# Two heads in one operand: mirrored odd heads in the level products of a recurrent mixer

## The chip, the cores and the metric

The kernel runs on one core of a Trainium2 chip. The time is the device time of one execution in microseconds (us); the figure compared is the median of several executions. The core has a matrix engine (TensorE, PE in the profile; its weight loads are PEld), a vector engine (VectorE, DVE), a scalar engine (ScalarE, ACT), GpSimd (POOL) and a queue engine that issues most transfers (SyncE, SP). Each works through its own instruction list in order and waits for the others by semaphores. TensorE reads its two operands from the on-chip memory (SBUF) and writes to the accumulators (PSUM), which DVE and ACT read.

## The reference

One inference step of a two-layer decoder: 1024 prompt tokens and 8 sample tokens share the weights, model width 1024, everything in float32. Layer 0 mixes tokens by a gated linear recurrence (HGRN2) with four heads of 128 beside cross-attention into 256 memory tokens, layer 1 by stick-breaking attention; each layer ends with a SwiGLU network of width 2816. The change touches the recurrence, whose prompt part is

```python
def a_mixer(hn, w_in, lb, hg_gain, mem_k, mem_v, w_o, s0):
    q_h, f_h, i_h, g_h, q_m = jnp.split(hn @ w_in, 5, axis=-1)
    q = jax.nn.silu(q_h).reshape(B, L, HG_HEADS, HG_DK)
    logf = jnp.logaddexp(jnp.log(lb), jnp.log1p(-lb) + jax.nn.log_sigmoid(f_h.astype(jnp.float32)))
    k = -jnp.expm1(logf)
    v = i_h.reshape(B, L, HG_HEADS, HG_DV)
    o, S = hgrn2_scan(q, k, v, logf, s0)
...
def hgrn2_scan(q, k, v, logf, s0):          # one step over a chunk
    b = jnp.cumsum(fi, axis=2)
    o_inter = jnp.einsum('bhtk,bhkv->bhtv', qi * jnp.exp(b), S)
    rel = b[:, :, :, None, :] - b[:, :, None, :, :]
    dec = jnp.exp(jnp.where(causal, rel, -jnp.inf))
    att = jnp.einsum('bhtk,bhsk,bhtsk->bhts', qi, ki, dec)
    o = o_inter + jnp.einsum('bhts,bhsv->bhtv', att, vi)
    S_new = jnp.exp(b_last[:, :, 0, :, None]) * S + jnp.einsum('bhsk,bhsv->bhkv', ki * jnp.exp(b_last - b), vi)
```

The score of a query at time t for a key at an earlier time s is a sum over 128 channels of q, k and the product of all forget gates f between s and t; each channel has gates of its own, so `att` is not one matrix product. After the mixer comes a norm per head and an output gate, then the output projection.

## The kernel before, in words

The prompt is done in two groups g of G = 512 tokens; the second also carries the 8 sample tokens (width WID = 520). Activations lie with channels on the 128 partitions and time along the free axis. A float32 projection (`proj`, L274) is three matmuls per weight block: weights are split into a rounded part (ACT, L260) and a remainder (DVE, L261), and rounded x rounded, rounded x remainder and remainder x rounded are summed. A projection of one head takes 8 weight blocks, so 24 matmuls of 512 columns.

The recurrence of a group is `hgrn_prompt` (called `core` of the mixer). The four heads go in two pairs hp; the tiles `Ft`, `Kt`, `Qt` hold gates, keys and queries of a pair, head hh = 0 or 1 in the middle index. A chunk is 128 time steps, CH = 4 of them in a group. First the diagonal of each chunk (L1160, four matmuls of 128 columns for each head, times the identity into the score tile `atts`). Then seven levels, lv = 0 to 6, with m = 1, 2, 4, ... 64: a chunk is cut into blocks of 2m, and the late half's queries meet the early half's keys, each already multiplied by the gates to the border between the halves. Only the late half's queries are read, 64 columns of a chunk, with a step. For one level and one pair these are 8 matmuls (L1180: two heads, four chunks) into one PSUM tile `s`. Afterwards DVE extends the products: late queries times the gate product of the early half (L1185), early keys times that of the late half (L1186), and the gate products of the merged blocks (L1187). `copy_predicated` (L1190) writes those rows of the PSUM tile that belong to the block into `atts`, under `mask`, one table for each level, which POOL makes at the kernel's start with two `affine_select` each (L163, L166) and DVE casts (L169).

The end of the core goes head by head ("tail" below): K is transposed (L1201), copied by ACT to `kT` (L1203), multiplied with V (L1207), chunk by chunk the scores meet V (L1215) and the carried state meets Q (L1219), while DVE moves the state on (L1220, L1224); then square (ACT, L1226), a sum over channels by a matmul with ones (L303), Ln and Exp on ACT (L304, L305), and the scaled output (DVE, L1228).

What else TensorE does meanwhile is set by `weave`: it takes generators with weights and steps the one that is furthest behind its weight. Group 0's core is woven with a chain: the memory tokens' load, keys (`mem_keys`, L812, transposes L820) and values (`mem_values`, L839, its splits L835 and L836) of layers 0 and 1, and last the memory queries `qm`, four projections of 24 matmuls, evacuated at L1232. Group 1's core is woven with a part of group 0's SwiGLU network. Tiles come from rotating pools (PSUM `s` 3 buffers, score and other tiles `b` 7, temporaries `t` 3, split weights `ws` 5), and a scheduler sets the final order of each engine's instructions within these dependences.

At the start (`start`, L373) four blocks of 128 tokens are loaded (`xtok`), DVE and ACT form sums of squares (L366 on DVE, L368 on ACT), ACT the reciprocal roots (L369, L370), DVE scales the block (L371), TensorE transposes it (L396) and ACT evacuates (L399). The first projection rows (L1048, splits at L1043) need all four blocks. The masks of POOL and DVE are made in the same microseconds, as are the page indices `pidx` (POOL, L207 and L208).

Of the kernel before, what the change touches and what calls it, by code (L numbers as in the profile page):

```python
# [9 lines left out]
F32 = mybir.dt.float32  # L10
# [14 lines left out]
def tile_decoder(  # L25
# [46 lines left out]
    def nm(s):  # L72
        uid[0] += 1
        return f"{s}_{uid[0]}"
# [62 lines left out]
    make_identity(nc, ident)  # L137
    ones = const.tile([P, P], F32, name="ones")
    nc.vector.memset(ones, 1.0)
    epsb = const.tile([P, 1], F32, name="epsb")  # L140
    nc.vector.memset(epsb, EPS)
    trif = const.tile([P, P], F32, name="trif")
# [11 lines left out]
        compare_op=ALU.is_equal, fill=0.0, base=0, channel_multiplier=0,  # L154
    )

    mask = const.tile([P, 7, 64], U8, name="mask")
    for lv in range(7):
        m = 1 << lv
        nb = 64 // m  # L160
        mf = tpool.tile([P, nb, m], F32, tag="t", name=nm("mf"))
        src = ones[:, 0:64].rearrange("p (b m) -> p b m", m=m)
        nc.gpsimd.affine_select(  # L163
            mf, src, pattern=[[-2 * m, nb], [0, m]], compare_op=ALU.is_ge, fill=0.0, base=0, channel_multiplier=1
        )
        nc.gpsimd.affine_select(  # L166
            mf, mf, pattern=[[2 * m, nb], [0, m]], compare_op=ALU.is_ge, fill=0.0, base=m - 1, channel_multiplier=-1
        )
        nc.vector.tensor_copy(mask[:, lv, :], mf.rearrange("p b m -> p (b m)"))  # L169

    xsraw = const.tile([P, ND, NB], F32, name="xsraw")
    par = const.tile([P, P], F32, name="par")
# [57 lines left out]
            yield from g_  # L230

    def weave(*streams):

        live = [[0, n, g_] for g_, n in streams]
        while live:
            cur = min(live, key=lambda e: e[0] / e[1])
            cur[0] += 1
            try:
                next(cur[2])
            except StopIteration:  # L240
                live.remove(cur)


    def pv(ps, g):
# [35 lines left out]
    def split_to(dst, src):  # L280
        nc.scalar.copy(dst[0], src)  # L281
        nc.vector.tensor_sub(dst[1], src, dst[0].bitcast(F32))  # L282

    def silu(dst, ps, g):

# [771 lines left out]
    def v_proj(g, W, m0, xt, vt, vs):  # L1057
        vt.extend((C(), C()) if g else (A(), A()))
        if not g:
            yield from rows_proj(W, m0, xt, vt)  # L1060
            return
        for h in range(H):
            ps = proj(g, W, 0, ND, m0 + h * P, xt)
            t = T()
            nc.scalar.copy(sv(t, g), pv(ps, g))
            to_token(t, vt, h)
            if g:
                nc.vector.tensor_copy(vs[:, h, :], t[:, G : G + NB])
            yield

    def gate_proj(g, W, xt, Ft, Kt):
        n = NG[g]
        for h in range(H):
            if h % 2 == 0:
                Ft.append(A())
                Kt.append(A())
            ps = proj(g, W, 0, ND, 4 * P + h * P, xt)
            f = T()
            nc.scalar.copy(sv(f, g), pv(ps, g))
            e = T()  # L1080
# [7 lines left out]
            nc.scalar.activation(Fd, e[:, :n], AF.Exp)  # L1088
            nc.scalar.activation(Kd, f[:, :n], AF.Exp)
# [63 lines left out]
    def hgrn_prompt(g, Ft, Kt, Qt, Vt):  # L1153
        atts = []
        for h in range(H):
# [10 lines left out]
            atts.append(at)  # L1166
            nc.vector.tensor_mul(Q_[:, :G], Q_[:, :G], Ft[h // 2][:, h % 2, :G])
            yield
        for lv in range(7):
            m = 1 << lv  # L1170
            nbg = G // (2 * m)
            for hp in range(2):
                F_, K_, Q_ = Ft[hp], Kt[hp], Qt[hp]
                pl = S()
                plv = pl.rearrange("p (h c n) -> p h c n", h=2, c=CH)
                for hh in range(2):
                    for c in range(CH):
                        cs = slice(c * P, (c + 1) * P)
                        rhs = Q_[:, hh, cs].rearrange("p (b t m) -> p b t m", t=2, m=m)[:, :, 1, :]
                        nc.tensor.matmul(plv[:, hh, c, :], K_[:, hh, cs], rhs, start=True, stop=True)  # L1180
                for hh in range(2):
                    Qv = Q_[:, hh, :G].rearrange("p (b t m) -> p b t m", t=2, m=m)
                    Kv = K_[:, hh, :G].rearrange("p (b t m) -> p b t m", t=2, m=m)
                    Fv = F_[:, hh, :G].rearrange("p (b t m) -> p b t m", t=2, m=m)
                    nc.vector.tensor_mul(Qv[:, :, 1, :], Qv[:, :, 1, :], Fv[:, :, 0, 0:1].to_broadcast([P, nbg, m]))  # L1185
                    nc.vector.tensor_mul(Kv[:, :, 0, :], Kv[:, :, 0, :], Fv[:, :, 1, 0:1].to_broadcast([P, nbg, m]))  # L1186
                    nc.vector.tensor_mul(Fv[:, :, 0, 0:1], Fv[:, :, 0, 0:1], Fv[:, :, 1, 0:1])  # L1187
                nb = 64 // m
                for hh in range(2):
                    nc.vector.copy_predicated(  # L1190
                        atts[hp * 2 + hh].rearrange("p (c b t m) -> p c b t m", c=CH, t=2, m=m)[:, :, :, 1, :],
                        mask[:, lv, :].rearrange("p (b m) -> p b m", m=m).unsqueeze(1).to_broadcast([P, CH, nb, m]),
                        pl[:, hh * 256 : (hh + 1) * 256].rearrange("p (c b m) -> p c b m", c=CH, m=m),
                    )
                yield
        for h in range(H):
# [13 lines left out]
            for c in range(CH):  # L1210
                cs = slice(c * P, (c + 1) * P)
                has = not (g == 0 and c == 0)
                cur = carry[:, h, :] if c == 0 else Sa[:, (c - 1) * P : c * P]
                nxt = carry[:, h, :] if c == CH - 1 else Sa[:, cs]
# [13 lines left out]
            nc.vector.scalar_tensor_tensor(F_[:, :G], po, hgn, r, op0=ALU.mult, op1=ALU.mult)  # L1228
            yield

    def scaled_evac(dst, ps, g):
# [2 lines left out]
    class mixer_a:  # L1234
# [5 lines left out]

        def fq(self):
            yield from gate_proj(self.g, self.W, self.xt, self.F, self.K)
            yield from heads2(self.g, self.W, 0, self.xt, silu, A, self.Q)

        def v(self):
            yield from v_proj(self.g, self.W, 8 * P, self.xt, self.V, self.vs)
# [198 lines left out]
    def store_y(g, R):  # L1445
# [113 lines left out]
```

## Time and profile before

| | |
|---|---|
| median of 3 runs | 2497.12 us (2493.58 to 2499.96) |
| profiled execution, its time | 2499.1 us |
| its span | 2497.4 us |
| granted TensorE clock, mean | 0.997 |
| busy: PE / DVE / ACT / POOL | 99% / 63% / 47% / 4% |
| level matmuls (L1180), busy | 53.3 us in 448 records |

A float32 matmul leaves two records in the trace, so 448 records are 224 matmuls. In a table of groups each row is a source line, the engine, the operation, the tiles (written, then read), their shapes and the count, then the busy time in us and the mean of one in ns, then the idle time of the engine just before them and what ended it. In the chain that ended last each row has the start, the length, and what held the end: an instruction group, a transfer, or "issue", where no wait is shown. In the timeline each row has start and length of a run of one operation; lengths of neighbours overlap a little, since instructions are pipelined.

### The profile page before, as it was taken

Reading aid. Unit: us, or ns where it says so; the run is one execution under the profiler, and the core shown is the slowest. Engines: PE = TensorE matmul, PEld = TensorE weight load, DVE = VectorE, ACT = ScalarE, POOL = GpSimd, SP = SyncE. Lnnn points to the kernel's source line nnn. Section 1 sums busy time; section 2 is a strip of 40 time slices with the busy share of each in tenths; the row PEclk is TensorE's granted clock in tenths of the full one; section 3 lists DMA queues with packets and bytes.
Section 4 is the critical chain, followed back from the end, with each engine's and each line's share of the span. In section 5 each row is a group of like instructions: output and inputs, shape, how many; then the busy total and the mean of one; then the engine's idle time right before and its main releaser. Section 6 shows DMA issues by size and latency. Waiting matters only on the chain.

```text
span 2497.4 us, 40764 instructions
## 1 busy us (share of the span) xinstructions
PE 2462.8 (99%) x15565; PEld 2169.9 (87%) x15565; DVE 1571.8 (63%) x2756; ACT 1183.0 (47%) x2277; POOL 98.3 (4%) x139
## 2 busy tenths in 40 slices
PE   8999999999999999999999999999999999999998
PEld 6888988877877897999999989877787797999997
DVE  5766556655765585655544575777577648755655
ACT  5446543243433454555433454555444445564444
POOL 1000000000000000010111100022000000000000
PEclk9999999999999999999999999999999999999999
DMA  5352252233643447586678976544454234365542
GB/s 186 114 165 68 72 156 81 60 110 116 184 124 98 129 138 227 156 195 177 173 191 215 234 193 196 160 142 138 121 149 130 85 115 122 121 192 145 151 137 69
DMA packets 496110, 358.21 MB, mean 143 GB/s; under 512 B 19110, under 2 KB 443635, under 8 KB 495915
## 3 DMA queue, kind: packets, MB, share of 16 engines
q1 hardware_dynamic: 477354, 301.08, 40.5%
q0 software_dynamic: 18560, 54.53, 9.1%
q8 instruction: 122, 2.00, 0.3%
q14 instruction: 74, 0.60, 0.1%
HBM read 325.73 MB, written 75.94 MB: 161 GB/s over the span
## 4 chain that ended last, share of the span: by engine, by line
PE 88%; DVE 5%; DMA 3%; ACT 2%; issue 2%; POOL 0%; SPq 0%; DVEq 0%; ACTq 0%; POOLq 0%
PE mm L274 59%; PE q L552 7%; PE q L667 5%; PE s L1180 2%; PE q L510 2%; PE mm L1048 2%; PE s L903 1%; PE s L862 1%; PE mm L812 1%; DMA b<-qd 1%; PE mm L839 1%; DVE ws L261 1%; PE ns L957 1%; PE s L1336 1%; DMA c<-in_cache_sb_v,pidx 1%
## 5 line engine op out<-in xcount | busy, mean ns | idle before, releaser
L274 PE MATMUL mm<-x,ws 128*128 128x260 f32 (+1 forms) x7776 | 1332.9, 330 | 0.0
L274 PEld LDWEIGHTS mm<-x,ws 128*128 128x128 f32 x7776 | 1148.3, 188 | 151.5 <-issue 12.0
L260 ACT CAST ws<-w 128x512 fp32r<-128x512 f32 x712 | 420.2, 591 | 763.2 <-PE mm L274 620.2
L261 DVE TENSOR_TENSOR ws<-w,ws 128x512 fp32r<-128x512 f32 x712 | 462.5, 653 | 286.8 <-ACT ws L260 278.3
L274 PE MATMUL mm<-m,ws 128*128 128x512 f32 (+1 forms) x2112 | 393.5, 343 | 0.1
L274 PEld LDWEIGHTS mm<-m,ws 128*128 128x128 f32 x2112 | 324.4, 189 | 49.9 <-issue 2.6
L667 PE MATMUL q<-m,ws 128*128 128x260 f32 x1056 | 128.8, 283 | 0.0
L667 PEld LDWEIGHTS q<-m,ws 128*128 128x128 f32 x1056 | 127.2, 188 | 0.4 <-ACT hT L485 0.2
L543 DVE TENSOR_TENSOR ws<-w,ws 128x512 fp32r<-128x512 f32 x126 | 86.6, 691 | 61.5 <-ACT ws L542 59.3
L552 PE MATMUL q<-y,ws 128*128 128x260 f32 x864 | 112.9, 283 | 0.0
L542 ACT CAST ws<-w 128x512 fp32r<-128x512 f32 x126 | 78.0, 621 | 69.6 <-PE q L667 27.4
L552 PEld LDWEIGHTS q<-y,ws 128*128 128x128 f32 x864 | 107.6, 189 | 0.0
L291 DVE TENSOR_SCALAR t<-mm 128x512 f32<-128x512 f32 (+1 forms) x82 | 56.7, 692 | 79.6 <-PE mm L274 79.6
L447 DVE TENSOR_TENSOR r<-r,mm 128x512 f32<-128x512 f32 (+1 forms) x96 | 66.0, 688 | 61.1 <-PE mm L274 60.3
L703 DVE TENSOR_TENSOR t<-t,mm 128x512 f32<-128x512 f32 (+1 forms) x66 | 45.5, 690 | 74.2 <-PE mm L274 73.9
L295 DVE TENSOR_TENSOR t<-t,t 128x512 f32<-128x512 f32 (+1 forms) x66 | 45.8, 694 | 70.6 <-ACT t L294 70.6
L552 PE MATMUL q<-x,ws 128*128 128x260 f32 x648 | 86.3, 282 | 0.0
L552 PEld LDWEIGHTS q<-x,ws 128*128 128x128 f32 x648 | 81.3, 188 | 0.0
L314 DVE TENSOR_TENSOR st<-st,n 128x512 f32<-128x512 f32 (+1 forms) x98 | 67.1, 691 | 8.8 <-ACT n L313 7.0
L281 ACT CAST m<-t 128x512 fp32r<-128x512 f32 (+1 forms) x88 | 54.9, 624 | 18.1 <-DVE t L703 8.9
L282 DVE TENSOR_TENSOR m<-t,m 128x512 fp32r<-128x512 f32 (+1 forms) x88 | 61.0, 693 | 2.6 <-ACT m L281 1.4
L984 POOL DMA_INDIRECT c<-in_cache_sb_k,pidx x16 | 16.4, 1026 | 1170.5 <-ACT n L313 958.6
(339 smaller groups left out, 2557.9 us busy)
## 6 DMA issues: line engine op xcount, KB each, us to landing
w<-in_w_gu SPq DMA_DIRECT2D x334, 256.0 KB, 3.4
w<-in_w_down SPq DMA_DIRECT2D x160, 256.0 KB, 3.5
w<-in_w_in_a SPq DMA_DIRECT2D x80, 256.0 KB, 3.0
wsum<-in_w_gu POOLq DMA_DIRECT2D x18, 1024.0 KB, 9.5
w<-wsum SPq DMA_DIRECT2D x72, 256.0 KB, 3.8
w<-in_w_o SPq DMA_DIRECT2D x64, 256.0 KB, 2.8
wsum<-in_w_gu POOLq DMA_DIRECT2D x12, 1280.0 KB, 10.7
w<-in_w_mem_kv SPq DMA_DIRECT2D x32, 256.0 KB, 3.2
```

Source lines behind the costliest of these rows:

```text
L260: nc.scalar.copy(ws[:, 0, :n, :], raw[:, :n, :])
L261: nc.vector.tensor_sub(ws[:, 1, :n, :], raw[:, :n, :], ws[:, 0, :n, :].bitcast(F32))
L274: nc.tensor.matmul(ps[:, a, : PW[g]], wt, xt[k][:, xi, o : o + PW[g]], start=(k == 0 and wi == 0), stop=(k == nk - 1 and wi == 2),)
L281: nc.scalar.copy(dst[0], src)
L282: nc.vector.tensor_sub(dst[1], src, dst[0].bitcast(F32))
L291: nc.vector.tensor_scalar(sv(x, g), pv(ps, g), -44.0, None, op0=ALU.max)
L314: nc.vector.tensor_add(acc[:, :n], acc[:, :n], t[:, :n])
L447: nc.vector.tensor_add(dst, dst, pv(ps, g))
L542: nc.scalar.copy(w[:, 0, :], src)
L543: nc.vector.tensor_sub(w[:, 1, :], src, w[:, 0, :].bitcast(F32))
L552: nc.tensor.matmul(ps[:, :h], w[:, wj, k * P : (k + 1) * P], x[:, xi, :], start=(first and k == 0 and wi == 0), stop=(k == 3 and wi == 2), ...
L667: nc.tensor.matmul(pp[a][:, :h], wt, mids[k][:, xi, a * h : (a + 1) * h], start=(k == 0 and wi == 0), stop=(k == nf - 1 and wi == 2),)
```

## The change

Odd heads are stored mirrored in time. Where the even head's late halves stand, the odd head's early halves stand. One tile `x` of a pair then holds, for a level, the even head's keys in the early positions and the odd head's keys in the late positions, and is the stationary operand for both heads at once: a level and pair is four matmuls (L1260) with 128 moving columns, 64 late queries of the even head and 64 of the odd one. For the next level `move` builds the next `x` in a second tile `z`: one ACT copy (L1238) and two DVE products (L1243, L1244; copies at L1240 and L1241 ahead of the first level), which take the place of the key products. The late queries of both heads are one DVE operation (L1265), the gate products one (L1269). The predicated copy (L1280) stays for m below 32 with a mask for each side (14 masks, L169, L173, L177); at m = 32 and 64 ACT copies the blocks by partition range (L1275): four operations on 32 partitions for a pair at m = 32 and two on 64 partitions at m = 64.

To mirror, gates, keys and queries of odd heads are written with a negative step (`rev`, `put`, `silu_heads`); V of group 0, which lies with time on the partitions, is turned by four matmuls with the anti-diagonal matrix `flip` and copied back; in group 1 the transposing copy reads in reverse. In the tail the odd heads go through the chunks in reverse order, and the output is written in reverse, so that what follows is as before. `weave` gets its loop from `mixed`, a generator; group 0's memory queries no longer come after the memory keys and values but are mixed among them, 4 steps to 18.

Lines that move: L274 becomes L286, L303 to L305 become L338 to L340, L366 and L371 become L401 and L406, L812 and L839 become L847 and L874, L1048 becomes L1083, L1201, L1203 and L1207 become L1291, L1293 and L1297, L1215 and L1219 become L1306 and L1310, L1226 and L1228 become L1317 and L1322.

```diff
+    flip = const.tile([P, P], F32, name="flip")
+    nc.gpsimd.affine_select(
+        flip, ones, pattern=[[1, P]], compare_op=ALU.is_equal, fill=0.0, base=1 - P, channel_multiplier=1
+    )
...
-    mask = const.tile([P, 7, 64], U8, name="mask")
+    mask = const.tile([P, 7, 2, 64], U8, name="mask")
...
+        for side in range(2):
+            o = side * m
...
+    def rev(ap):
+        st, n = ap.ap[-1]
+        return bass.AP(ap.tensor, ap.offset + (n - 1) * st, [list(d) for d in ap.ap[:-1]] + [[-st, n]])
+
+    def put(dst, src, h, g, op):
+        n = NG[g]
+        if h % 2 == 0:
+            op(dst[:, :n], src[:, :n])
+            return
+        op(dst[:, :G], rev(src[:, :G]))
+        if g:
+            op(dst[:, G:n], src[:, G:n])
...
         if not g:
             yield from rows_proj(W, m0, xt, vt)
+            odd = [t[:, :, :512].rearrange("p c (e o d) -> p c e o d", o=2, d=P)[:, :, :, 1] for t in vt]
+            pts = [S(), S()]
+            for c in range(CH):
+                r = CH - 1 - c
+                nc.tensor.matmul(
+                    pts[c // 2][:, (c % 2) * 256 : (c % 2) * 256 + 256], flip, odd[r // 2][:, r % 2],
+                    start=True, stop=True,
+                )
...
+        def move(F_, x, y, z, m):
...
+            nc.scalar.copy(view(z, *swap), view(y, *swap))
...
+            nc.vector.tensor_mul(view(z, *keep), view(x, *keep), view(F_, *fk))
+            nc.vector.tensor_mul(view(y, *swap), view(x, *swap), view(F_, *fs))
...
-                plv = pl.rearrange("p (h c n) -> p h c n", h=2, c=CH)
+                for c in range(CH):
+                    o = c * P
+                    nc.tensor.matmul(
+                        pl[:, o : o + P], x[:, o : o + P],
+                        view(Q_, o + m, [WID - m, 2], [2 * m, nb], [1, m]), start=True, stop=True,
+                    )
+                late = view(Q_, m, [WID - m, 2], [2 * m, nbg], [1, m])
+                nc.vector.tensor_mul(late, late, view(F_, 0, [WID + m, 2], [2 * m, nbg], [0, m]))
+                move(F_, x, Kt[hp][:, 1, :G], z, m)
+                xs[hp], zs[hp] = z, x
...
-                for hh in range(2):
-                    for c in range(CH):
-                        cs = slice(c * P, (c + 1) * P)
-                        rhs = Q_[:, hh, cs].rearrange("p (b t m) -> p b t m", t=2, m=m)[:, :, 1, :]
-                        nc.tensor.matmul(plv[:, hh, c, :], K_[:, hh, cs], rhs, start=True, stop=True)
...
+                    if m >= 32:
+                        w = 2 * m
+                        for o in range(0, P, w):
+                            rows, late = slice(o + hh * m, o + hh * m + m), o + (1 - hh) * m
+                            nc.scalar.copy(
+                                atts[hp * 2 + hh].rearrange("p (c n) -> p c n", c=CH)[rows, :, late : late + m],
+                                pl.rearrange("p (c h n) -> p c h n", c=CH, h=2)[rows, :, hh, o // 2 : o // 2 + m],
+                            )
+                        continue
...
-        (chain(mem_load(), mem_keys(0), mem_values(0), mem_keys(1), mem_values(1), a0.qm(M)), 22),
+        (mixed((chain(mem_load(), mem_keys(0), mem_values(0), mem_keys(1), mem_values(1)), 18), (a0.qm(M), 4)), 22),
```

The order of the instructions changes in four stretches: at the start (DVE, POOL), where V is flipped, and along the two cores. Behind group 1's core it is as before.

DVE at the start, before: mask casts (`mask<-mf`), the small terms of the forget bound (`lb`, `lbt`), the sum of squares of the last token block that DVE does itself (L366), and the scaling of the last two blocks (L371). The number behind a tile's name is its allocation.

```order
L169 CAST mask<-mf_147 128x64
L169 CAST mask<-mf_151 128x64
L169 CAST mask<-mf_155 128x64
L191 RECIPROCAL lb<-lbt 128x4
L192 TENSOR_TENSOR lbt<-lbt,lb 128x4
L193 TENSOR_TENSOR lb<-lbt 128x4
L366 ISA c_223,rr_222<-xtok_106 128x1024
L366 ISA rr_222 128x1
L194 TENSOR_SCALAR oml<-lb 128x4
L200 COPY biass<-biasp 128x32 x2
L371 TENSOR_SCALAR xtok_106<-xtok_106,rr_216 128x1024
```

And after, from the tenth mask on:

```order
L177 CAST mask<-mf_169 128x64
L201 TENSOR_TENSOR lb<-lbt 128x4
L401 ISA c_253,rr_252<-xtok_106 128x1024
L401 ISA rr_252 128x1
L177 CAST mask<-mf_173 128x64
L177 CAST mask<-mf_177 128x64
L177 CAST mask<-mf_181 128x64
L202 TENSOR_SCALAR oml<-lb 128x4
L208 COPY biass<-biasp 128x32 x2
L406 TENSOR_SCALAR xtok_106<-xtok_106,rr_246 128x1024
L177 CAST mask<-mf_185 128x64
L406 TENSOR_SCALAR xtok_106<-xtok_106,rr_252 128x1024
```

Ten masks, not seven, now stand ahead of the last sum of squares, three behind it, and the fourteenth between the two last scalings. On POOL the selects of that one stand behind the two operations on `pidx`, those of the other thirteen ahead of them.

TensorE in group 0's levels, before: each unit of 8 level matmuls is followed by 12 matmuls of the memory values (`ws` is the split weight, `memt` the memory tokens).

```order
L1180 MATMUL s_1114<-a_709,a_531 128x64 x8
L839 MATMUL mm_1091<-ws_1133,memt_801 128x512 x6
L839 MATMUL mm_1091<-ws_1144,memt_801 128x512 x6
L1180 MATMUL s_1153<-a_626,a_435 128x64 x8
L839 MATMUL mm_1091<-ws_1172,memt_802 128x512 x6
L839 MATMUL mm_1091<-ws_1183,memt_802 128x512 x6
L1180 MATMUL s_1192<-a_709,a_531 128x64 x8
```

And after, about the same place (`a_475`, `b_988` and so on are the two tiles that take turns as `x`; `mm_1361` is a memory query projection):

```order
L1260 MATMUL s_1266<-a_749,b_989 128x128 x4
L874 MATMUL mm_1209<-ws_1280,memt_842 128x512 x6
L874 MATMUL mm_1209<-ws_1291,memt_842 128x512 x6
L1260 MATMUL s_1300<-a_666,a_475 128x128 x4
L874 MATMUL mm_1209<-ws_1314,memt_843 128x512 x6
L874 MATMUL mm_1209<-ws_1325,memt_843 128x512 x6
L1260 MATMUL s_1338<-a_749,a_571 128x128 x4
L286 MATMUL mm_1361<-x_263,ws_1353 128x512 x3
L286 MATMUL mm_1361<-x_271,ws_1353 128x512 x3
```

A unit is four matmuls of twice the columns, and where a query projection comes in, 24 matmuls stand between two units.

TensorE in group 0's tail, before, from the sum of squares of one head (L303) to the product of the next head's `kT` (L1207):

```order
L303 MATMUL s_1732<-b_1730,ones 128x512
L274 MATMUL mm_1747<-x_265,ws_1744 128x512
L274 MATMUL mm_1747<-x_273,ws_1744 128x512 x3
L274 MATMUL mm_1747<-x_281,ws_1744 128x512 x3
L274 MATMUL mm_1747<-x_289,ws_1744 128x512 x3
L1201 MATMUL s_1773<-ident,a_531 128x128 x4
L274 MATMUL mm_1816<-x_233,ws_1808 128x512 x3
L274 MATMUL mm_1816<-x_241,ws_1808 128x512
L1207 MATMUL s_1780<-a_292,b_1778 128x128 x2
```

And after:

```order
L338 MATMUL s_1721<-b_1719,ones 128x512
L874 MATMUL mm_1671<-ws_1739,memt_841 128x512 x3
L1291 MATMUL s_1748<-ident,a_475 128x128 x4
L874 MATMUL mm_1671<-ws_1782,memt_842 128x512 x4
L1297 MATMUL s_1755<-a_322,b_1753 128x128 x2
```

Where 10 to 15 matmuls of the memory queries stood ahead of the transposes, three of the second layer's memory values stand.

More of the change, by code (lines that the diff above doesn't have):

```diff
@@ L1209, in hgrn_prompt @@
             po = S()
-            for c in range(CH):
+            for i in range(CH):
+                c = CH - 1 - i if h % 2 else i
                 cs = slice(c * P, (c + 1) * P)
-                has = not (g == 0 and c == 0)
-                cur = carry[:, h, :] if c == 0 else Sa[:, (c - 1) * P : c * P]
-                nxt = carry[:, h, :] if c == CH - 1 else Sa[:, cs]
+                has = not (g == 0 and i == 0)
+                cur = carry[:, h, :] if i == 0 else Sa[:, (i - 1) * P : i * P]
+                nxt = carry[:, h, :] if i == CH - 1 else Sa[:, i * P : (i + 1) * P]
                 nc.tensor.matmul(
@@ L1242, in fq @@
             yield from gate_proj(self.g, self.W, self.xt, self.F, self.K)
-            yield from heads2(self.g, self.W, 0, self.xt, silu, A, self.Q)
+            for h in range(H):
+                if h % 2 == 0:
+                    self.Q.append(A())
+                ps = proj(self.g, self.W, 0, ND, h * P, self.xt)
+                silu_heads(self.Q[-1][:, h % 2, :], ps, self.g, h)
+                yield
         def v(self):
```

104 lines of the change are left out of this document (75 added, 29 removed).

## The prediction

> **What bounds the kernel now.** I read the page first, then the groups of instructions, then the chain that ended last, then the busy time by stretches around the two places that change.
>
> ```profile
> PE 2462.8 (99%) x15565; PEld 2169.9 (87%) x15565; DVE 1571.8 (63%) x2756; ACT 1183.0 (47%) x2277; POOL 98.3 (4%) x139
> ...
> PE 88%; DVE 5%; DMA 3%; ACT 2%; issue 2%; POOL 0%; SPq 0%; DVEq 0%; ACTq 0%; POOLq 0%
> ```
>
> TensorE is the bound: 99% busy, 88% of the chain. So PE time taken out is time won as long as VectorE (DVE) and ScalarE (ACT) keep feeding it. Busy time of PE is modelled, hence I price matmuls by the pitch in the chain, where runs of them stand start to start; its columns are start, length, what, records.
>
> ```profile
> 90.35 1.73 PE s L1180 x16
> ...
> 104.52 2.84 PE mm L812 x24
> ...
> 112.06 1.73 PE s L1180 x16
> 113.80 2.82 PE mm L839 x12
> 116.61 1.73 PE s L1180 x16
> ...
> 403.51 1.78 PE s L1160 x16
> ...
> 484.16 5.30 PE s L1180 x48
> ```
>
> ```profile
> L1180 PEld LDWEIGHTS s<-a,a 128*128 128x128 f32 x448 | 53.4, 192 | 1.3
> L1180 PE MATMUL s<-a,a 128*128 128x64 f32 x448 | 53.3, 271 | 0.0
> ...
> L1160 PE MATMUL s<-a,a 128*128 128x128 f32 x64 | 8.4, 276 | 0.7 <-DVE a L295 0.7
> ```
>
> A level unit (one level, one head pair) is 8 matmuls, each two records: 16 records in 1.73 us, 108 ns a record, at m = 1 (90.35, every second element read) and late in group 1 alike (5.30 / 48 = 110 ns). The 128-column matmuls of L1160 take 1.78 / 16 = 111 ns a record. So 64 columns cost what 128 cost, and half of what a level streams is wasted. 448 records are 28 units: 7 levels, 2 pairs, 2 groups.
>
> Next, who feeds PE there (columns: sum and count for PE, PEld, DVE, ACT, POOL, then clock, DMA share, GB/s):
>
> ```profile
> 85.00:95.00 10.00, 9.31 (x83) 9.09 (x83) 9.68 (x20) 4.61 (x10) 0.00 (x0) 1.00 0.13 46
> 95.00:112.00 17.00, 17.00 (x134) 16.05 (x132) 15.66 (x36) 7.22 (x15) 0.00 (x0) 1.00 0.56 169
> ...
> 147.00:167.00 20.00, 20.00 (x123) 17.37 (x122) 15.04 (x41) 6.36 (x10) 0.00 (x0) 1.00 0.51 154
> ...
> 430.00:450.00 20.00, 20.00 (x130) 17.91 (x128) 17.82 (x41) 6.24 (x10) 0.00 (x0) 1.00 0.16 46
> ```
>
> From 95 us on PE is full, but DVE is 75 to 92% busy (15.04 of 20, 15.66 of 17): the reserve is thin, and it is the question of this case.
>
> **The change, part by part.**
>
> *Level products.* 4 matmuls of 128 columns take the place of 8 of 64: 8 records at 111 ns = 0.89 us for 1.73 us. 28 x 0.84 = 23.6 us less. Upper bound, a record at 108 ns: 28 x 0.866 = 24.2 us. Lower bound: the moving operand is now two strided runs of 128 columns together; no row shows such a read. If it streams at half the rate of L1160, a record costs 2 x 111 = 222 ns, a unit 1.78 us, and the saving is gone (1 us lost). I take 111 ns, since the strided 64 columns at m = 1 show no surcharge, though a surcharge could hide there below the 108 ns. The Trainium skill (TensorE: Matmul & The Clock Gate, section Back-to-back issue gap) gives the warm gap of a single matmul as columns / 2.4 + 2.5 ns, that is time by streamed columns; by it 64 columns cost about half of 128, the unit's time would not change and the sum would be about +6. The trace's 108 against 111 ns speaks against it, and I follow the trace.
>
> *DVE and ACT in the levels.* One unit before, at m = 4, with the copies of the unit ahead of it (columns: start, length; the pitch is from start to start):
>
> ```profile
> 114.89 1.32 DVE L1190 COPY_PREDICATED b<-mask,s 128x256 f32<-128x256 uint8 x2
> 115.99 1.33 DVE L836 TENSOR_TENSOR ws<-w,ws 128x512 fp32r<-128x512 f32 x2
> 117.49 0.42 DVE L1185 TENSOR_TENSOR a<-a,a 128x256 f32<-128x256 f32 x1 [0.17 <-PE s L1180]
> 117.83 0.42 DVE L1186 TENSOR_TENSOR a<-a,a 128x256 f32<-128x256 f32 x1
> 118.17 0.28 DVE L1187 TENSOR_TENSOR a<-a 128x64 f32<-128x64 f32 x1
> 118.38 0.43 DVE L1185 TENSOR_TENSOR a<-a,a 128x256 f32<-128x256 f32 x1
> ...
> 119.25 0.75 DVE L1190 COPY_PREDICATED b<-mask,s 128x256 f32<-128x256 uint8 x2
> 119.92 1.28 DVE L261 TENSOR_TENSOR ws<-w,ws 128x512 fp32r<-128x512 f32 x2
> ```
>
> The products stay the same in elements: two 256-element ones (0.34 each) become one of 512 (1.28 / 2 = 0.64, by the split's row), two others (L1186, 2 x 0.34) stay, the two small F products (0.21) become one of 128 (about 0.3). The copies (0.67 a unit; 1.10 at m = 1 and 2, since 115.99 follows 114.89) go to ACT at m = 32 and 64 only. Counted from the order between the first and the last level unit of group 0, with these pitches:
>
> - PE before: 112 level matmuls x 0.216, 24 transposes x 0.222, 192 of 256 columns x 0.118 (2.84 / 24), 84 of 512 x 0.235 (2.82 / 12) = 72 us.
> - PE after: 56 x 0.222, 14 x 0.222, 144 x 0.118, 120 x 0.235 (72 of them queries) = 61 us.
> - DVE after: 14 x (0.64 + 0.68 + 0.3), copies 4 x 1.10 + 6 x 0.67, 25 splits x 0.64, 7 evacuations x 0.34 = 50 us.
>
> So DVE is at 82% over the stage: no wait as a whole. A unit between two value stages has 0.89 + 2.82 = 3.71 us of PE against 0.64 + 0.68 + 0.3 + 0.67 + 1.28 = 3.57 of DVE, just enough; the query projections (24 x 0.235 = 5.6 us of PE for two splits, 1.28 us) let DVE catch up. ACT gets 16 half-tile copies and 12 block copies a group. By L873's 128x256 row (0.471 each) that is at most 13 us, in a stretch where it is 32 to 42% busy. Queued behind them are split casts, whose tiles are made a matmul run or more ahead. I charge 0.6 us for the beginning (85 to 95, where DVE is at 97% and PE already loses 0.7) and 0.6 for short waits in group 1.
>
> ```profile
> L873 ACT ACTIVATE b<-s,nmx 128x256 f32<-128x256 f32 x64 | 29.8, 471 | 21.2 <-DVE nmx L867 21.2
> ```
>
> *The flip.* Four 128x256 f32 matmuls. Four such matmuls' records:
>
> ```profile
> 1929.08 0.87 PE s L862 x4
> ```
>
> 0.217 a record, 8 records: +1.7 us of PE. Its four copies lie beside the gate projections that stand around it: nothing.
>
> *Start.* POOL now makes 14 masks and the flip matrix, DVE casts 14. Before, the start ran over POOL and DVE alternately:
>
> ```profile
> 10.52 0.25 POOL mf L166
> 10.79 0.19 DVE mask L169
> ...
> 12.86 0.67 DVE xtok L371
> ...
> 15.68 1.86 PE mm L1048 x4
> ```
>
> ```profile
> L166 POOL TENSOR_SCALAR_AFFINE_SELECT mf<-mf 128x64 f32<-128x64 f32 x7 | 3.2, 464 | 0.1
> L163 POOL TENSOR_SCALAR_AFFINE_SELECT mf<-ones 128x64 f32<-128x64 f32 x7 | 2.4, 356 | 3.0 <-PE s L174 1.8 <-DVE mask L169 1.2
> L207 POOL TENSOR_SCALAR pidx<-ptb 128x16 int32<-128x16 int32 x1 | 1.2, 1152 | 0.8 <-DMA ptb<-in_page_table 0.8
> L208 POOL TENSOR_TENSOR pidx<-pidx,iot 128x16 int32<-128x16 int32 x1 | 0.8, 765 | 0.1
> ```
>
> In the new order three more casts stand ahead of the last block's sum of squares on DVE: 3 x 0.45 (0.20 + 0.25, the two selects' pitch in the chain) = 1.4 us. And the fourteenth cast stands ahead of the last scaling of xtok; its selects stand on POOL behind the two page index operations (1.2 + 0.8), which came in no one's way before. That is another 1.0 to 1.8. I take +2.8 us; bounds 0 (POOL ahead of DVE throughout) and 4.2 (7 x 0.45, and a third of an index operation more). Nothing covers it: the first matmul of L1048 needs all four blocks.
>
> *Group 0's tail.* Before, each head had 24 query matmuls around its chain; now 12 of values(1).
>
> ```profile
> 169.53 3.23 PE mm L274 x14
> 172.76 0.44 PE s L1201 x4
> 173.20 0.94 PE mm L274 x4
> ```
>
> ```profile
> L304 ACT ACTIVATE b<-s,epsb 128x512 f32<-128x512 f32 x4 | 2.8, 689 | 2.8 <-PE s L303 2.8
> L305 ACT ACTIVATE b<-b 128x512 f32<-128x512 f32 x4 | 2.5, 632 | 0.1
> ...
> L1203 ACT COPY b<-s 128x512 f32<-128x512 f32 x4 | 2.3, 584 | 0.0
> ```
>
> After the sum of squares (L303, now L338) of one head stood 3.23 us of queries ahead of the next head's K transposes; now 3 x 0.235 = 0.7. The copy of kT (L1203, now L1293) therefore stands on ACT right behind Ln and Exp of the head before: 0.69 + 0.63 + 0.58 = 1.9 us from L338's end. PE comes to the products that need kT (L1297) after 0.7 + 0.44 + 0.94 = 2.1 us. So it just fits. Bounds 0 and 0.5 us a head (one of ACT's other operations in between), three heads; I take 0.1 each, +0.3.
>
> *Without price.* Reversed reads and writes of ACT and DVE (same instructions, negative step, beside projections); eight-column extra pieces in group 1, some 8 at 0.2 us on engines with room there. Off the path by the same cover; if a negative step halved their speed, about 16 operations of 0.6 us would still lie beside PE's projections.
>
> Sum: -23.6 + 1.7 + 2.8 + 0.6 + 0.6 + 0.3 = -17.6 us. The profiled execution took 2499.1 us (span 2497.4), so 2481.5; it stood 2.0 above the median 2497.1, against which the forecast is 2479.5, say 2480.
>
> **The rivals.**
>
> *DVE becomes the bound in the levels.* For: 92% at 95 to 112 and 89% at 430 to 450; at m = 1 and 2 the predicated copies are dearer, so such a unit asks 0.64 + 0.68 + 0.4 + 1.10 + 1.28 = 4.1 us for PE's 3.71. Against: the sum over the stage, 50 against 61. If each of group 0's 14 units waits 0.4 us and each of group 1's 0.25, 9 us come back: 2489.
>
> *The strided read is dear.* For: nothing in the trace excludes it, since the weight load hides up to 108 ns. Against: m = 1 costs what later levels cost. At half rate a unit saves nothing: 28 x (1.78 - 1.73) + 6.0 = +7.4, 2504.5; it decides the sign where a unit gains 17.6 / 28 = 0.63 us less, 79 ns on each of 8 records, that is from 190 ns a record. The Trainium skill (SBUF — State Buffer, section Door 1) says that a strided float32 read is free as long as two accesses fall in each 16-byte line, which a step of two elements keeps; no run here shows it. The rule by columns cited above would end nearly there, at 2497.1 + 6.0 = 2503, and by L1180's row it has no more than 0.01 of this case's chance.
>
> *The start is hidden.* POOL's selects are short and its queue may run ahead of DVE: then -20.4, 2476.7.
>
> **How the numbers follow.** Forecast, with the upper-bound case that lies beside it: 0.65; start hidden 0.08; DVE bound 0.17; strided read 0.10. A measurement of this kernel tells about 0.3%, 7.5 us, from no change: faster is below 2489.6. Forecast and hidden start are faster (0.73), of the DVE case a little under a third (0.05), the rest of it is the same (0.12); of the strided case half stays within 7.5 us (0.05) and half, with a read worse than half rate, does not. Faster 0.78, same 0.16, slower 0.06. The forecast's own range is 2476 to 2485 (saving 24.2 and start 0.5, against the tail at 1.5, the start at 4.2 and the beginning at 3.0); to leave out no more than 2 in 10 it is carried into the DVE case: 2473 to 2494.
>
> **What would show it.** Right: in the chain, L1260 with 8 records in about 0.89 us at every level; the first L1083 matmul at 18.0 to 19 us; PE at 100% from the second level on. Wrong: L1260 records over 150 ns, most at small m; or DVE over 95% between the levels with PE waiting on L1243, L1244 or on a split; or heads of group 0's tail more than 0.5 us apart from PE's sum.

## The result, and the profile after

The changed kernel takes 2479.22 us (median of 6 runs, 2477.2 to 2482.94); the kernel before, in the same session, 2497.03 us. The ratio is 0.9928, 95% interval 0.9915 to 0.9941: 17.8 us less, where 17.6 were forecast and 2480 us predicted. By the interval the gain lies between 14.7 and 21.2 us. The profiled execution took 2479.36 us, its span 2477.6.

The page of the changed kernel:

```profile
PE 2442.6 (99%) x15349; PEld 2147.9 (87%) x15349; DVE 1567.4 (63%) x2703; ACT 1201.4 (48%) x2341; POOL 102.7 (4%) x154
...
PE 93%; DVE 3%; ACT 1%; DMA 1%; issue 1%; SPq 0%; POOL 0%; DVEq 0%; ACTq 0%
```

TensorE remains the bound, with 216 records less: 448 level records became 224, and the flip brought 8. First the timeline of PE at m = 1 of group 0 (start, length), then the chain in group 0's levels from m = 2 on and at the end of group 1's:

```profile
109.31 0.85 PE L1260 MATMUL s<-a,b 128*128 128x128 f32 x6
109.99 0.38 PE L855 MATMUL mm<-ident,t 128*128 128x128 f32 x2
```

```profile
120.89 0.91 PE s L1260 x8
...
128.53 0.89 PE s L1260 x8
129.42 2.76 PE mm L874 x12
132.18 0.89 PE s L1260 x8
...
140.44 5.55 PE mm L286 x24
145.99 0.89 PE s L1260 x8
...
468.64 2.90 PE s L1260 x24
```

A level unit stands at 0.89 us for 8 records, 111 ns a record, from m = 2 up; at m = 1 six records take 109.99 - 109.31 = 0.68 us, 113 ns each, and group 1 ends with 2.90 / 24 = 121 ns. The stretched read of two strided runs costs next to nothing against the 111 ns of a contiguous one (L1160 in the kernel before). The stage from the first to the last level unit of group 0, in the same columns as before:

```profile
109.30:170.00 60.70, 60.15 (x397) 54.55 (x396) 49.20 (x108) 28.94 (x62) 0.00 (x0) 1.00 0.59 177
```

That is 60.7 us with 49.2 us of DVE; counted from the order, 61 and 50 were expected. The waits of PE up to 500 us, by who was waited for (total, times, longest):

```profile
PE ns L431 <- DVE xtok L406: 8.7, 4, 4.6
PE s L182 <- POOL mf L173: 5.1, 1, 5.1
PE mm L855 <- ACT t L852: 0.6, 1, 0.6
PE s L1297 <- ACT b L1293: 0.2, 1, 0.2
PE mm L847 <- DVE memt L294: 0.2, 1, 0.2
```

Three short ones lie in group 0's core, 1.0 us in all where the kernel before had 0.7; the longest, 0.6, ends at 114.67, in the second unit of m = 1, and behind it PE is full up to the tail. None lies in group 1's. The big ones are the start, and its chain reads

```profile
13.42 1.25 DVE c L401
...
16.85 0.76 DVE xtok L406
...
18.91 2.08 PE mm L1083 x4
20.98 0.85 PE ns L431 x4
21.84 0.85 PE mm L1083 x2
...
45.39 1.62 PE mm L286 x7
47.01 1.76 PE s L1100 x8
```

The first projection comes at 18.91 us, 3.2 later than the 15.68 of before. The flip (L1100) takes 1.76 us.

Where the time went, by places that both kernels pass. In the kernel before these stand in the chain (the transposes of group 1's sample tokens; two late waits on `qd`):

```profile
217.65 0.59 PE s L386 x8
...
704.33 4.49 DMA b<-qd
...
1873.64 5.08 DMA b<-qd
```

and in the changed kernel

```profile
212.61 0.59 PE s L421 x8
...
687.51 4.18 DMA b<-qd
...
1853.82 4.94 DMA b<-qd
```

| place | before | after | difference |
|---|---|---|---|
| first projection at the start | 15.68 | 18.91 | +3.2 |
| first projections of the heads (L274, L286) | 40.61 | 45.39 | +4.8 |
| sample tokens' transposes, behind group 0's core | 217.65 | 212.61 | -5.0 |
| first wait on `qd`, behind group 1's core | 704.33 | 687.51 | -16.8 |
| last wait on `qd` | 1873.64 | 1853.82 | -19.8 |
| span | 2497.4 | 2477.6 | -19.8 |

The step from +3.2 to +4.8 is told apart from the change further down (the queries spread in the kernel before). Between the second and the third row lie the flip (+1.76) and 14 level units (-11.8): -10.0, measured -9.8. Between the third and the fourth lie the other 14: -11.8, measured -11.8. The last 3.0 us of this pair of profiles arise where both kernels do the same; the profiled execution of before stood 2 us above its median, and that of after 0.1, so about two thirds of them can be put down to that pair of executions; the last microsecond stays open.

### The profile page after: what moved, and what is told of

Same layout as the page of the kernel before. It is cut to its first block, busy times and chain, and to the rows that moved or that the text cites. A ratio compares the mean times of both kernels' runs of the same rounds, so it can differ in the third digit from the quotient of the medians.

```text
span 2477.6 us, 40360 instructions
## 1 busy us (share of the span) xinstructions
PE 2442.6 (99%) x15349; PEld 2147.9 (87%) x15349; DVE 1567.4 (63%) x2703; ACT 1201.4 (48%) x2341; POOL 102.7 (4%) x154
## 4 chain that ended last, share of the span: by engine, by line
PE 93%; DVE 3%; ACT 1%; DMA 1%; issue 1%; SPq 0%; POOL 0%; DVEq 0%; ACTq 0%
PE mm L286 63%; PE q L587 7%; PE q L702 5%; PE q L545 2%; PE mm L1083 2%; PE s L938 1%; PE s L897 1%; PE s L1435 1%; PE s L1260 1%; PE ns L992 1%; PE mm L874 1%; PE s L1474 1%; PE mm L847 1%; PE s L924 1%; PE s L1462 1%
## 5 line engine op out<-in xcount | busy, mean ns | idle before, releaser
L286 PE MATMUL mm<-x,ws 128*128 128x260 f32 (+1 forms) x7776 | 1330.6, 330 | 0.0
L286 PEld LDWEIGHTS mm<-x,ws 128*128 128x128 f32 x7776 | 1148.0, 188 | 150.8 <-issue 10.4
L286 PE MATMUL mm<-m,ws 128*128 128x512 f32 (+1 forms) x2112 | 392.5, 343 | 0.0
L286 PEld LDWEIGHTS mm<-m,ws 128*128 128x128 f32 x2112 | 324.5, 189 | 50.0 <-issue 2.1
L326 DVE TENSOR_SCALAR t<-mm 128x512 f32<-128x512 f32 (+1 forms) x74 | 51.2, 692 | 64.0 <-PE mm L286 63.9
L1019 POOL DMA_INDIRECT c<-in_cache_sb_k,pidx x16 | 16.4, 1024 | 1148.4 <-DMA out_sbv_prompt<-c 936.9
```

Of the source, the lines that this page charges most:

```text
L286: nc.tensor.matmul(ps[:, a, : PW[g]], wt, xt[k][:, xi, o : o + PW[g]], start=(k == 0 and wi == 0), stop=(k == nk - 1 and wi == 2),)
L326: nc.vector.tensor_scalar(sv(x, g), pv(ps, g), -44.0, None, op0=ALU.max)
```

## The experiments

The kernel before was run again beside each set; its medians there were 2497.4, 2498.34 and 2497.51 us, so distances to the changed kernel's 2479.22 carry about a microsecond from that.

**The level products split again.** The merged operand stays, but each matmul of 128 columns is issued as two of 64.

```diff
-                    nc.tensor.matmul(
-                        pl[:, o : o + P], x[:, o : o + P],
-                        view(Q_, o + m, [WID - m, 2], [2 * m, nb], [1, m]), start=True, stop=True,
-                    )
+                    for h0 in range(2):
+                        nc.tensor.matmul(
+                            pl[:, o + h0 * 64 : o + h0 * 64 + 64], x[:, o : o + P],
+                            view(Q_, o + m + h0 * (WID - m), [2 * m, nb], [1, m]), start=True, stop=True,
+                        )
```

> The changed kernel, but each of the level matmuls of 128 columns is given as two of 64 columns with the same stationary operand; everything else stays, mirrored storage, copies and queries among them. Theory (a float32 matmul record costs about 110 ns at 64 columns as at 128): a level unit goes back from 8 records to 16, 28 x 0.84 = +23.6 us, about 2503 us, the unit 1.73 us in the chain. Rival (the time follows the streamed columns): the unit stays at 0.89 us and the time at 2479 us.

Measured: 2502.55 us (2498.92 to 2504.35), 23.3 us above the changed kernel. Its chain:

```profile
120.77 1.74 PE s L1261 x16
122.50 2.89 PE mm L847 x24
```

The unit is back at 1.74 us and the whole of the saving is gone. So the saving follows the number of records, at 64 columns as dear as at 128. What sets the 108 to 111 ns, the load of a stationary operand that goes with each record or something else, was not tried. This kernel is slower than the one before by 5.2 us of median (ratio 1.0019, 1.0009 to 1.0029), about what the start (3.2) and the flip (1.8) cost with no saving to pay for them.

**The memory queries last.** One part of the change undone.

```diff
-        (mixed((chain(mem_load(), mem_keys(0), mem_values(0), mem_keys(1), mem_values(1)), 18), (a0.qm(M), 4)), 22),
+        (chain(mem_load(), mem_keys(0), mem_values(0), mem_keys(1), mem_values(1), a0.qm(M)), 22),
```

> The changed kernel with the memory queries behind the memory keys and values again, as in the kernel before. Theory (DVE has just enough time even between value stages): between the first and the last level unit of group 0 PE has 58 us of work (12.4 level, 3.6 transposes, 22.7 keys, 19.7 values) against 52 us on DVE; only the four units at m = 1 and 2 wait some 0.4 us each, and the tail gets its cover back: 0 to +2 us, 2479 to 2481 us. Rival (DVE is the bound in the levels once the queries are gone): 14 units wait 0.4 us, +5.6 us, 2485 us.

Measured: 2484.75 us (2482.35 to 2485.53), 5.5 above the changed kernel, the rival's number. Its waits, and its busiest stretch on DVE:

```profile
PE ns L830 <- issue: 1.4, 1, 1.4
PE mm L847 <- DVE memt L294: 0.7, 2, 0.5
PE s L1215 <- DVE a L317: 0.7, 1, 0.7
PE mm L847 <- ACT memt L293: 0.5, 1, 0.5
PE mm L855 <- ACT t L852: 0.4, 1, 0.4
```

```profile
86.00:100.00 14.00, 11.31 (x70) 9.52 (x68) 10.95 (x20) 8.01 (x16) 0.00 (x0) 1.00 0.26 72
...
120.00:140.00 20.00, 20.00 (x140) 18.50 (x139) 19.73 (x43) 8.96 (x18) 0.00 (x0) 1.00 0.59 184
```

DVE is indeed full between 120 and 140 us, 19.73 of 20, and the chain of this run leads through it from 115.9 to 134 us; yet PE loses only 0.4 us where it comes back to PE, at 142 (L855). PE's idle time lies at the core's beginning: 2.7 us between 86 and 100, where the changed kernel has 0.2 up to 104, and the first four rows of waits, 3.3 us, all end before 104. There DVE and ACT still make the last queries and the memory tokens' splits. By the sample tokens' transposes this profile is 3.8 us behind that of the changed kernel (216.38 for 212.61), and at the first wait on `qd` still 3.8 (691.28 for 687.51); the rest of the 5.5 arises where both kernels do the same. So the median meets the rival's number partly by chance, and the place is not the rival's. Hence the next run.

**One query ahead, three behind.** Only the first query projection stays where the changed kernel has it (`one_of` takes one projection of the generator, `rest_of` the other three).

```diff
+    qm0 = a0.qm(M)
...
-        (mixed((chain(mem_load(), mem_keys(0), mem_values(0), mem_keys(1), mem_values(1)), 18), (a0.qm(M), 4)), 22),
+        (mixed((chain(mem_load(), mem_keys(0), mem_values(0), mem_keys(1), mem_values(1), rest_of(qm0)), 21), (one_of(qm0), 1)), 22),
```

> The changed kernel with one memory query projection at the place of its first one (among the diagonal products ahead of the levels), and the other three behind all memory values. With all four last 5.5 us were lost, 3.8 of them by the start of group 1's tokens at 216 us, of which the waits of PE show 2.7 us between 86 and 100 us and 1.0 later. Theory (the first query is the cover of the core's beginning, and that is what the spreading is worth): most of it comes back, 2480 to 2481 us, with the first waits gone and the mark at 212.6 to 213.6 us. Rival (DVE is the bound within the levels): less than 1 us comes back, 2484 us, and the waits move into the levels.

Measured: 2480.52 us (2478.39 to 2482.05). The sample tokens' transposes come at

```profile
211.77 0.59 PE s L421 x8
```

against 212.61 in the changed kernel and 216.38 with all queries last. Of the 0.8 us by which it is ahead of the changed kernel, the start gave 1.2 (the heads' projections began at 44.18 for 45.39), so from there on it lost 0.4. Nearly all of what spreading the queries is worth, 3.8 us by the traces, therefore comes from the first one, whose 5.6 us of PE work cover the beginning of the core; the three among the levels are worth nothing that these runs can tell (+1.3 us of median, ranges overlapping).

**The queries spread in the kernel before.** The same line alone, put into the kernel before.

> The kernel before with nothing but its memory queries spread among the levels (4 steps to 18). Theory (a unit of 1.73 + 2.82 us leaves DVE its time, so nothing is to be won in the levels; only the wait of 0.7 us at the beginning goes): -1 to 0 us, 2496 to 2497 us. Rival (the spreading itself is worth what it is worth in the changed kernel, 5.5 us): 2492 us.

Measured: 2496.86 us (2494.62 to 2501.09); ratio 0.9998 (0.9988 to 1.0007). No difference, as the theory had it: the wait of 0.7 us at L1160 was gone from its trace, and that is too little to be seen. In the kernel before the beginning held only that wait; the new order with the queries last holds the same 0.7 (now at L1215) and 2.6 us more, and the first query is what covers them.

This run also shows something of the start, which its edit does not touch. Its chain there:

```profile
15.60 2.08 PE mm L1052 x4
17.68 0.85 PE ns L400 x4
```

The first projection comes at 15.60, as in the kernel before (15.68), but the four transposes behind it took 0.85 us where they took 0.44 there, and the heads' projections began at 41.97, not at 40.61. From the first projection to the heads' it is 24.9 us in one execution and 26.4 in the other, with the same instructions; the changed kernel's 26.5 is that of the slower one.

**Predicated copies at all levels.**

```diff
-                    if m >= 32:
+                    if m >= 128:
```

> The changed kernel with predicated copies on DVE at all levels, none on ScalarE; queries spread as changed. Theory (with the queries among the levels DVE has room): 2.7 us more on DVE per group in stretches where it is 65 to 90% busy, so within 1 us of 2479 in either direction, no new wait of PE before 560 us. Rival (the copies on ScalarE are what keeps DVE from being the bound): 16 units of m = 32 and 64 wait up to 0.67 us less what slack is there, +3 to +5 us, with waits of PE on DVE in the levels.

Measured: 2479.26 us (2478.46 to 2480.42), the changed kernel's own time. ScalarE's copies at the two highest levels bring nothing that this run can tell: DVE had the room, and no wait of PE on it is new. Together with the queries last:

> The changed kernel with the queries last again and with predicated copies on DVE at m = 32 and 64 too, no block copies on ScalarE: the mirrored level products alone. Theory: DVE goes from 52 to 55 us against 58 us of PE in group 0's levels, so it still fits, with +1 to +3 us of short waits, 2480 to 2482 us. Rival (DVE is the bound): eight units more wait 0.67 us each beside the 14 x 0.4, about +9 us in all, 2488 us.

Measured: 2482.67 us (2481.06 to 2484.33), 0.7 above the theory's range, far from the rival's 2488, and not to be told from the run with only the queries last. The mirrored level products alone are 14.7 us faster than the kernel before (2497.4 beside this run); the 3.1 us missing to 17.8 fit the cover that the first query gives.

**The masks in the kernel before.** 14 masks and their casts, with only the first side used.

> The kernel before with 14 masks made in place of 7, only the first side used. Theory (the masks hold the start): the first matmul of L1048 moves from 15.7 to 18 to 19 us, as in the changed kernel, and the time by as much, +2.5 to +3.3 us, 2500 us. Rival (what comes behind catches up, as the levels of the changed kernel with late masks partly did): 0 to +1 us.

Measured: 2500.96 us (2499.55 to 2506.05) against 2498.34 of the kernel before; ratio 1.0012 (1.0003 to 1.0022): 2.6 us more, as the theory had it, though the interval (0.8 to 5.5 us) just reaches the rival's +1. The start moves as in the changed kernel, where the first projection came at 18.91:

```profile
18.94 0.79 PE mm L1052
```

**The masks late.** The ten masks that are still used (m below 32) are made after the first gate head has been issued.

```diff
-    for lv in range(7):
...
-    drain(a0.v(), a0.fq())
+    drain(a0.v())
+    fq = a0.fq()
+    next(fq)
+    for lv in range(5):
...
+    drain(fq)
```

> The changed kernel, with the ten masks that are still used made only after the first gate head has been issued, so that none stands on POOL or DVE during the start. Theory (the masks stand in the chain to the first projection, and nothing covers them): the first L1083 matmul comes at 13.5 to 15 us in place of 18.9, -4 to -5.4 us, 2474 to 2475 us, below the start of the kernel before too (15.7). Rival (the start is held by the token blocks' transfers, by ACT's sums or by the weights): the start stays above 17 us, and the time within 2 us of 2479.

Measured: 2475.63 us (2474.31 to 2476.31), 3.6 less than the changed kernel, a little short of the 4 to 5.4 that the theory had. The start, the stretch of the chain where the rest was lost, and the wait that is new there:

```profile
14.26 2.08 PE mm L1066 x4
...
104.48 5.85 DMA out_mk_prompt<-t
...
111.52 7.10 PE mm L269 x24
```

```profile
PE mm L838 <- ACT t L835: 2.0, 1, 2.0
```

The first projection comes at 14.26 us, 4.65 earlier. But then the core begins earlier than the store of memory keys to HBM, begun at 104.48, can free the tile `t`; ACT's next copy into it waits, and PE loses 2.0 us at the keys' transposes (L838). It loses 1.5 more right behind: the 24 matmuls of a query projection at 111.52 take 7.10 us, where the changed kernel's (at 115.33) took 5.56, and the granted clock fell, to 0.50 between 113 and 115. In the windows from 112 to 130 us, of this run and of the next one, which has no such wait (the column ahead of the last two is the clock), it reads

```profile
112.00:130.00 18.00, 18.00 (x99) 15.63 (x99) 14.52 (x31) 6.28 (x13) 0.00 (x0) 0.91 0.42 119
```

```profile
112.00:130.00 18.00, 18.00 (x121) 16.37 (x120) 16.86 (x37) 7.51 (x16) 0.00 (x0) 1.00 0.53 150
```

The heads' projections had begun 5.9 us earlier than in the changed kernel (39.45 for 45.39); by the sample tokens 2.3 of it were left. More of the queries early cover the wait:

```diff
-18), (a0.qm(M), 4)), 22),
+18), (a0.qm(M), 8)), 22),
```

> The changed kernel with the masks made after the first gate head, and the queries spread over the first half of the levels (8 steps to 18, so two or three stand early). Theory (the wait of 2.0 us that the late masks showed at the memory keys, on a tile whose store was still under way, goes when more queries stand ahead of it; the later levels then lack cover): 2473 to 2477 us, against 2475.6. Rival (DVE is the bound in the later levels without queries): +3 us, 2479.

Measured: 2472.42 us (2470.89 to 2475.29), ratio to the kernel before 0.9897 (0.988 to 0.9913), and the wait is gone from its trace; no wait of PE on DVE came in the later levels. This beats both kernels, by 25.9 us of median and by 6.8.

**The fourth block's sum on ScalarE.** What stretches POOL's mask operations?

```diff
-            rms_rows(xtok[g][:, tb, :], P, g == 0 and tb % 2 == 1)
+            rms_rows(xtok[g][:, tb, :], P, g == 0 and tb == 1)
```

> The changed kernel with the sum of squares of the fourth token block on ScalarE in place of DVE. It tests what stretches POOL's mask operations: in the changed kernel one select of 64 elements took 1.22 us while DVE ran this sum, 0.2 to 0.3 us otherwise. Theory (a long DVE operation on SBUF holds POOL up): no select takes over 0.8 us at 13 to 15 us, unless it lies beside a scaling of xtok, and the first L1083 matmul comes 0.5 to 1.5 us earlier than 18.9. Rival (it is the select's own pattern or position): the same select, the first of the twelfth or thirteenth mask, still takes over 1 us.

The changed kernel's timeline (start, length):

```profile
13.35 1.33 DVE L401 CUSTOM_DVE_ANT_0 c<-xtok 128x1024 f32<-128x1024 f32 x1
```

```profile
13.36 0.24 POOL L173 TENSOR_SCALAR_AFFINE_SELECT mf<-mf 128x64 f32<-128x64 f32 x1
13.55 1.22 POOL L169 TENSOR_SCALAR_AFFINE_SELECT mf<-ones 128x64 f32<-128x64 f32 x1
...
15.16 0.29 POOL L215 TENSOR_SCALAR pidx<-ptb 128x16 int32<-128x16 int32 x1
...
15.70 0.69 POOL L169 TENSOR_SCALAR_AFFINE_SELECT mf<-ones 128x64 f32<-128x64 f32 x1
```

and with the sum on ScalarE

```profile
13.47 0.80 DVE L406 TENSOR_SCALAR xtok<-xtok,rr 128x1024 f32<-128x1024 f32 x1
```

```profile
13.68 0.69 POOL L169 TENSOR_SCALAR_AFFINE_SELECT mf<-ones 128x64 f32<-128x64 f32 x1
...
14.99 0.23 POOL L169 TENSOR_SCALAR_AFFINE_SELECT mf<-ones 128x64 f32<-128x64 f32 x1
```

```profile
17.79 2.08 PE mm L1083 x4
```

The same select took 1.22 us beside the long sum and ended at 14.77, 0.09 after it; now it lies beside a scaling that ends at 14.27 and itself ends at 14.37. The select of the fourteenth mask shows it the other way round: it took 0.69 beside a scaling in the changed kernel (15.70 to 16.39, the scaling 15.56 to 16.30), and 0.23 in this run, where nothing long stood beside it (14.99). So the length follows the DVE operation beside a select, and not the select's pattern or place. Not every overlap holds POOL up: the select at 13.36, which began within 0.01 us of the sum, took 0.24. The first projection came 1.1 us earlier. The 2475.59 us are a single execution, and no worth of the edit is read from them.

## Why the prediction was right

*Level products.* Right in mechanism and size: 111 ns a record, 0.89 us a unit, and the two groups' stretches come out at -9.8 (with the flip) and -11.8. The split run gives 23.3 us for the forecast 23.6. The rule by columns and the rival of the dear strided read both fall by these rows.

*The flip.* 1.76 us for 1.7.

*The start.* The mechanism was right, the size a little too small. The term was +2.8; the first projection came 3.2 later, and 14 masks in the kernel before moved it by 3.3 and the median by 2.6. By the heads' projections the difference was 4.8, since PE's first work went at half pace for longer: the four transposes at 20.98 took 0.85 us, where the same four took 0.44 in the kernel before. The sum had nothing for this, but it is no part of the change as far as these runs tell: with the start of the kernel before, another execution shows 0.85 too. One reason given inside the term was wrong: the page index operations, priced 1.2 + 0.8 us, took 0.29 and about 0.2, since nothing long ran on DVE beside them; in the kernel before the first stood beside the last sum of squares (11.38 to 12.60 us, the operation 11.59 to 12.74). In their place a mask's select took 1.22 us beside the last sum of squares, which itself started 2.0 us later (13.35 for 11.38) and not 1.4.

*Waits.* The 0.6 at the beginning, 0.6 in group 1 and 0.3 in the tail were too much: of the -16.8 us behind group 1's core, -23.6 + 1.76 + 4.8 leave 0.2 for them all. The tail fitted as reckoned, with 0.2 us of wait at one head. So the start came 0.4 dearer than its term and the waits 1.3 cheaper, and the slow pace put 1.6 us on this pair of executions by chance. That the medians lie 17.8 apart and the sum said 17.6 is in part luck: the executions of each kernel scatter over some 6 us, and the interval of the gain is as wide.

*DVE as the bound.* Given 0.17, did not come. The count by order (50 of 61 us) was right to 1 us. Its single prices were not all: the products of `move` at m = 1 took 0.66 us for 256 elements, where 0.42 was the length before, some 2 us in all, and the stage had room for that. With the queries last the chain did run through DVE for some 18 us, and PE lost 0.4 us: the reserve was as thin as the prediction said.

*What the query term meant.* That query projections among the levels let DVE catch up was not the reason for which they matter: what counts is the first one, ahead of the levels, and the prediction had charged 0.6 us for the beginning without saying what covers it; without that cover the waits there are 3.3 us.

## What to carry to other kernels

A float32 matmul with 64 moving columns takes as long as one with 128 in this kernel, so work that fills only half a matmul is worth pairing, even at the price of mirrored storage and a flip; the proof is to issue the paired work in halves again. What a change adds once at the start can stand in the chain with no cover: here the seven added tables, four of which are never read, cost 2.6 us when put into the kernel before, and moving the ten that are read out of the start brought 3.6 us. After such a move look for the next tile that is not free in time, and put work that waits for nothing ahead of it: here a wait of 2.0 us cost 1.5 more by the slower pace behind it.

## What the runs showed of the hardware beyond that

Three of POOL's selects stood until a long DVE operation beside them ended: 1.22 us in place of 0.2 to 0.3 beside a sum of 1024 columns, and twice 0.69 beside a scaling, ending 0.09, 0.10 and 0.09 us after it. The Trainium skill (SBUF — State Buffer, section Who interferes with whom) says that DVE and GpSimd share a pair of ports that, for some kinds of DVE instruction, the one that starts first holds for a whole instruction while the other waits. These rows agree with it.

TensorE's first work after the idle stretch of the start ran at half pace, with a granted clock that the windows show as 1.00: 0.85 us for four transposes at 20.98 us against 0.44 later. How long that lasts differs between executions with the same start (0.44 and 0.85 for the same transposes above). Behind the wait of 2.0 us in the run with the late masks the windows do show it, with a clock of 0.50 from 113 to 115 us. The Trainium skill (TensorE: Matmul & The Clock Gate, section What's actually happening) describes a clock held at half until a window of activity has passed; the pace agrees, and the recorded clock shows it behind the wait but not at the start. No run here varied the idle stretch by itself.

DVE's two products of `move` took 0.64 to 0.66 us at m = 1, and 0.41 to 0.47 from m = 2 on, for the same 256 elements; the second of them at m = 1 and m = 2 in the timeline of the changed kernel:

```profile
105.13 0.66 DVE L1244 TENSOR_TENSOR a<-b,a 128x256 f32<-128x256 f32 x1
...
114.05 0.41 DVE L1244 TENSOR_TENSOR a<-a,a 128x256 f32<-128x256 f32 x1
```

Why was not tried; the gate operand alternates between the two heads there element by element.
